# One decoder layer: the first two token groups projected without the row factor of RMSNorm, the factor multiplied in behind the projection

## The chip, the core and the metric

The kernel runs on one core of a Trainium2 chip. The metric is the device time of one execution in microseconds. The kernel before took 1266.46 us (median of three runs, 1264.92 to 1267.42). The core has five engines with one instruction queue each: TensorE (PE in the profile; PEld is its loading of weights), VectorE (DVE), ScalarE (ACT), GpSimd (POOL) and SyncE (SP), which issues most DMAs. TensorE writes to PSUM, in banks of 128 partitions by 512 words; the other engines copy results from there to SBUF.

## The reference, cut to what matters

```python
def rmsnorm(x, g):
    return x * rsqrt(mean(x * x, axis=-1) + EPS) * g

h = concatenate([meta, x])                      # 16 + 1024 tokens of 1024
a = rmsnorm(h, ln_mix_pre)
proj = a @ w_in                                 # 1024 x 3584
dq, dk, dv, hq, hf, hi, hg = split(proj)        # 7 kinds of 512 columns, 4 heads of 128 each
y_diff = diff_attention(dq, dk, dv, ...)        # relative-position bias, two softmaxes per head
y_hgrn = hgrn2(hq, hf, hi, hg, ...)             # gated linear recurrence, 4 heads
h = h + rmsnorm(concatenate([y_diff, y_hgrn]) @ w_out, ln_mix_post)
h = h + rmsnorm(conv_ffn(rmsnorm(h, ln_ffn_pre)), ln_ffn_post)
return h[16:]
```

All of it is f32. The factor `rsqrt(mean(x*x) + EPS)` is one number per token, the gain `g` one per column of x. Since the factor belongs to a token, `(x * g) @ w` may be multiplied by it afterwards; the gain may not.

## The kernel before, in words

**Precision.** Every f32 factor of a projection is split into a high part in the faster fp32r form and a low part, the rest. A projection is the sum of three products over eight slices k of 128 input columns: high weight by high x (`wh`, `ahi`), low weight by high x (`wl`, `ahi`), high weight by low x (`wh`, `alo`).

**Tokens.** The 1040 tokens (block 0 is the 16 meta rows, blocks 1 to 8 are 128 rows of x) form three groups: blocks 0 to 2 (272 tokens), 3 to 5 and 6 to 8 (384 each). Projections produce columns-by-tokens tiles: `pi_dq` is the PSUM accumulator of kind dq, one per group.

**The normed input.** x comes in twice. Its rows come as `x` (512 KB a block) and only serve to find the factors: the square and its sum per row (ScalarE with an accumulator, or DVE), then the reciprocal root on ScalarE. A transposed copy comes as `xr` (columns on the partitions), which is what TensorE needs. Since the factor there runs along the free dimension, it is spread over all partitions by TensorE: a diagonal matrix `dg` of the factors is multiplied with a matrix of ones into the PSUM tile `prs`. Then DVE forms `xr * gcol * prs` for each slice (`x_norm`, `gcol` is the gain), ScalarE casts it to `ahi`, and DVE or POOL subtracts to get `alo`. `ahi` and `alo` stay in SBUF for all 28 projection tiles.

**The start.** The loads are issued in a written order on SyncE's queue: blocks 1, 0, 2 of x, the first weight pieces (a kind has two of 256 KB; `wr` raw, cast into `wh` and `wl`) and group 0's transposed x, then blocks 3 to 5, the table for the position bias, group 1's transposed x, and later group 2's. Until the first data are there TensorE runs 26 and then 4 filler products of `ones`. Group 0's three kinds dq, dk, dv of head 0 come first, then group 1's, then group 2's. All instructions of this part keep the order in which they are written (the state "ordered"), on every engine. What a finished accumulator still needs is its evacuation, `out()`: for dq, ScalarE and DVE split it into the high and low parts of two half-heads (`q`); for dk the same into `k` and `kl`; for dv ScalarE copies it to `vt`, which TensorE later transposes into `avn` (`pn_va`, called by `flush()`). The position bias takes one product per head into PSUM (`pb`), a copy and a few steps on DVE.

**PSUM.** The start has eight banks: three tagged "ip" for the accumulators of groups 0 and 2, five tagged "m" for group 1's accumulators, `prs`, `pb`, `pn_va` and the fillers.

**The heads.** After the first three kinds the head stage begins with the projection `pi_hf` (it ends at about 470 us). It goes through four pairs of one attention head and one HGRN head; the projections of the next kind run between the steps of the current heads. Their evacuations go through the same functions: seven kinds in three groups per pair. Here DVE's, ScalarE's and POOL's order is set by a scheduler, TensorE's by the program.

**The rest.** From about 470 us on, the output projection, the convolutional feed-forward part and their norms run as before; the change does not touch them.

Of the kernel before, what the change touches and what calls it, by code (L numbers as in the profile page):

```python
# [36 lines left out]
WARM = 26  # L37
# [55 lines left out]
def layer_kernel(ctx: ExitStack, tc: tile.TileContext, x, meta, xt, relative, lbl, gpre, gpost, win,  # L93
# [23 lines left out]
    deep = {"ip": 3, "m": 5}  # L117
# [113 lines left out]
    at_p_cm, ap_ = pool("attn", 1, "right")  # L231
    z_cm, zp = pool("pre", 2, "right")
# [52 lines left out]
    def x_stats(g, on_vector=()):  # L285
        blks = range(*GROUPS[g])
        ss = zp.tile([P, 3], F32, tag="ss", name=f"ss{g}", bufs=3)
        if g == 0:
            V.memset(ss, 1.0)
        for c, i in sorted(enumerate(blks), key=lambda b: b[1] == 0):  # L290
            r = rows(i)
            if i in on_vector:
                V.tensor_tensor(x_rows[i][:r], x_rows[i][:r], x_rows[i][:r], op=ALU.mult)
                V.reduce_sum(ss[:r, c:c + 1], x_rows[i][:r], axis=AX.X)
            else:
                A.activation(x_rows[i][:r], x_rows[i][:r], AF.Square, accum_out=ss[:r, c:c + 1])
        rstd_of(ss, ss, D)
        res = {}
        for c, i in enumerate(blks):
            r = rows(i)  # L300
            res[i] = zp.tile([P, P], F32, tag="dg", name=f"dg{i}", bufs=3)
            if i in (1, 2, 3, 6):
                A.mul(res[i], ident, ss[:, c:c + 1])
            else:
                V.tensor_scalar(res[i][:r, :r], ident[:r, :r], ss[:r, c:c + 1], None, ALU.mult)
        return res

    def x_spread(g, stats):
        pt = ps_m(f"prs{g}")
        o = 0  # L310
        for i in range(*GROUPS[g]):
            r = rows(i)
            T.matmul(pt[:, o:o + r], ones[:r], stats[i][:r, :r], start=True, stop=True)
# [54 lines left out]
    def bias_table(h, tbb, oh):  # L368
        pt = ps_m(f"pb{h}")
        T.matmul(pt[:, :384], tbb[:, h], oh, start=True, stop=True)  # L370
        rb = zp.tile([P, 512], F32, tag=f"wv{h % 2}", name=f"rb{h}", bufs=1)[:, :384] if h > 1 else zp.tile([P, 384], F32, tag="rb", name=f"rb{h}", bufs=2)
# [34 lines left out]
    def hgrn_in(h):  # L406
# [15 lines left out]
        def ev_q(g, b0, b1, t0, t1, pt):  # L422
            A.mul(t["q"][:, t0:t1], pt, 128 ** -0.5)

        def ev_i(g, b0, b1, t0, t1, pt):
            ht = hp.tile([P, 384], F32, tag="ht", name=f"ht{h}_{g}", bufs=3)
            A.copy(ht[:, : t1 - t0], pt)
            late.append((t["vn"], ht, b0, b1, f"vh{h}_{g}"))

        def ev_g(g, b0, b1, t0, t1, pt):  # L430
            if g == 0:
                t["gate"] = hp.tile([P, L], F32, tag="gate", name=f"gate{h}")
            s = hp.tile([P, 384], F32, tag="sg", name=f"sg{h}_{g}")[:, : t1 - t0]
            sigmoid(s, s, pt)
            V.tensor_tensor(t["gate"][:, t0:t1], pt, s, op=ALU.mult)
# [196 lines left out]
    def attn_in(h):  # L632
# [8 lines left out]
        def ev_q(g, b0, b1, t0, t1, pt):  # L641
            for m in range(2):
# [4 lines left out]
        def ev_k(g, b0, b1, t0, t1, pt):  # L647
            for m in range(2):
# [158 lines left out]
    third = [ap_.tile([P, 4, 512], F32R, tag="pb", name=f"w3{c}", bufs=2) for c in range(2)]  # L807
# [17 lines left out]
    for i in (1, 0, 2):  # L825
        load_x(i)
    open_xt(1)
    load_raw(0, 0)
    load_xt(0, 0, 4)
    SY.dma_start(gcol, gpre)  # L830
# [4 lines left out]
    for i in (3, 4, 5):  # L835
        load_x(i)
    bias = spare[:64, 2 * D:2 * D + 388]
    SY.dma_start(bias, relative)
    for c in range(2):
        load_xt(1, 4 * c, 4 * c + 4)  # L840
    for c in range(2):
        for j in range(3):
            if j < 2:
                parts[j][c] = tuple(wp.tile([P, 512], F32R, tag=t, name=f"{t}_{tiles[j][1]}_{c}", bufs=4) for t in ("wh", "wl"))
            else:
                parts[j][c] = third[c][:, 0], third[c][:, 1]
# [35 lines left out]
    stats = x_stats(0, (0,))  # L882
    spread = {0: x_spread(0, stats)}
    keep_busy(warm, 4)
    w_hi(0, 0, G)
    w_lo(0, 0, G)
    w_hi(1, 0, G)
    w_lo(1, 0, G)
    for k in range(KD):
        x_norm(0, k, spread[0])  # L890
# [19 lines left out]
    for k in range(4):  # L910
        dq.mm(k, 0, ahi)
        dq.mm(k, 1, ahi)
        dk.mm(k, 0, ahi)
    for kd in (dq, dk):
        kd.part(1, 0, ahi)
    dk.part(0, 1, ahi)

    def low_parts(*ks):
        for k in ks:
            for kd in (dq, dk):  # L920
                kd.mm(k, 0, alo)

    for kd in (dq, dk):
        kd.part(1, 1, ahi)
    for half in range(2):
        dv.part(half, 0, ahi)
    low_parts(0, 1, 2, 3)
# [863 lines left out]
```

## Time and profile before

| | before |
|---|---|
| median of three runs | 1266.46 us (1264.92 to 1267.42) |
| the profiled execution | 1267.22 us |
| its span, first to last instruction | 1265.4 us |
| TensorE busy in the span | 1249.3 us (99%) |
| DVE, ScalarE, POOL busy | 911.9, 684.0, 512.9 us |
| mean granted TensorE clock | 0.998 |
| first product of a projection | at 11.69 us |
| head stage's first product (`pi_hf`) | at 51.08 us |

The span is what the profile sees; the execution's own time is 1.8 us longer. Times in the trace count from the span's start. In rows of an engine's order of time the columns are the start, the length, the engine, the line, the operation with its output and inputs by the program's names, the count of like instructions in a row, and in brackets how long the engine had waited ahead of it and for what. Line L60 is the helper through which every DVE, ScalarE and POOL operation passes, so those are told apart by their names; L863 is the product of a first-kind projection (`Kinds.mm`), L313 the spread product, L370 the bias product, L383 and L385 the transposes of dv, L250 to L254 the projections of the head stage.

### The profile page before, as it was taken

Reading aid. Unit: us, or ns where it says so; the run is one execution under the profiler, and the core shown is the slowest. Engines: PE = TensorE matmul, PEld = TensorE weight load, DVE = VectorE, ACT = ScalarE, POOL = GpSimd, SP = SyncE. Lnnn points to the kernel's source line nnn. Section 1 sums busy time; section 2 is a strip of 40 time slices with the busy share of each in tenths; the row PEclk is TensorE's granted clock in tenths of the full one; section 3 lists DMA queues with packets and bytes.
Section 4 is the critical chain, followed back from the end, with each engine's and each line's share of the span. In section 5 each row is a group of like instructions: output and inputs, shape, how many; then the busy total and the mean of one; then the engine's idle time right before and its main releaser. Section 6 shows DMA issues by size and latency. Waiting matters only on the chain.

```text
span 1265.4 us, 26124 instructions
## 1 busy us (share of the span) xinstructions
PE 1249.3 (99%) x10168; PEld 1169.8 (92%) x10168; DVE 911.9 (72%) x1505; ACT 684.0 (54%) x1632; POOL 512.9 (41%) x396
## 2 busy tenths in 40 slices
PE   9999999999999999999999999999999999999997
PEld 8999999999999998778999999999999998878886
DVE  6764646565655573557899888888898887797586
ACT  7765466547644764356764544445435454564554
POOL 5442323333313311353067676676776731020111
PEclk9999999999999999999999999999999999999999
DMA  8554564464634533787322221222222247955363
GB/s 323 171 105 100 97 140 84 98 125 116 117 100 68 126 88 123 235 276 262 114 68 71 89 93 59 101 76 76 94 76 83 76 130 269 354 171 166 92 217 125
DMA packets 117599, 169.30 MB, mean 134 GB/s; under 512 B 10258, under 2 KB 55122, under 8 KB 117476
## 3 DMA queue, kind: packets, MB, share of 16 engines
q1 hardware_dynamic: 94244, 156.10, 37.5%
q0 software_dynamic: 23232, 11.54, 7.7%
q8 instruction: 80, 1.31, 0.4%
q14 instruction: 43, 0.35, 0.1%
HBM read 138.50 MB, written 52.17 MB: 151 GB/s over the span
## 4 chain that ended last, share of the span: by engine, by line
PE 45%; DVE 5%; ACT 2%; issue 2%; POOL 1%; DMA 1%; SPq 0%; DVEq 0%; POOLq 0%; ACTq 0%
PE pd L1616 5%; PE pd L1617 5%; PE pd L1615 5%; PE pb L1438 4%; PE pb L1439 4%; PE pb L1440 4%; PE pa L1439 3%; PE pc L1440 3%; PE pa L1438 3%; PE pc L1439 3%; PE pc L1438 3%; PE pa L1440 3%; DVE t L60 1%; DVE xh L60 1%; DVE c L60 1%
## 5 line engine op out<-in xcount | busy, mean ns | idle before, releaser
L1438 PE MATMUL pb<-t,uh 128*128 128x258 f32 (+1 forms) x504 | 140.3, 278 | 0.9 <-DVE uu L60 0.9
L1439 PE MATMUL pb<-t,uh 128*128 128x258 f32 (+1 forms) x504 | 140.4, 279 | 0.4 <-DVE t L60 0.4
L1440 PE MATMUL pb<-t,ul 128*128 128x258 f32 (+1 forms) x504 | 139.9, 278 | 0.0
L1616 PE MATMUL pd<-wl,gh 128*128 128x512 f32 (+1 forms) x312 | 121.0, 388 | 1.7 <-DVE wl L60 1.7
L1615 PE MATMUL pd<-wh,gh 128*128 128x512 f32 (+1 forms) x312 | 120.7, 387 | 0.5 <-DVE x L60 0.5
L1617 PE MATMUL pd<-wh,gl 128*128 128x512 f32 (+1 forms) x312 | 120.7, 387 | 0.0
L60 ACT ACTIVATE c<-c 128x512 f32<-128x512 f32 x44 | 27.9, 634 | 150.5 <-DVE c L60 150.5
L60 DVE SCALAR_TENSOR_TENSOR c<-uu,cwt,c 128x512 f32<-128x512 f32 x88 | 105.6, 1200 | 0.0
L60 DVE SCALAR_TENSOR_TENSOR c<-ug,cwt,c 128x512 f32<-128x512 f32 x88 | 102.2, 1163 | 0.0
L1438 PEld LDWEIGHTS pb<-t,uh 128*128 128x128 f32 x504 | 94.7, 188 | 1.2 <-DVE uu L60 1.1
L60 POOL TENSOR_TENSOR ws<-ra,ra 128x512 f32<-128x512 f32 x42 | 70.7, 1682 | 61.9 <-DMA ra<-in_wup_dram 41.1
L1439 PEld LDWEIGHTS pb<-t,uh 128*128 128x128 f32 x504 | 94.8, 188 | 0.6 <-DVE t L60 0.6
L1440 PEld LDWEIGHTS pb<-t,ul 128*128 128x128 f32 x504 | 94.8, 188 | 0.0
L1439 PE MATMUL pa<-t,uh 128*128 128x258 f32 (+1 forms) x336 | 93.9, 279 | 0.0
L1438 PE MATMUL pa<-t,uh 128*128 128x258 f32 (+1 forms) x336 | 93.6, 278 | 0.0
L1440 PE MATMUL pa<-t,ul 128*128 128x258 f32 (+1 forms) x336 | 93.4, 278 | 0.0
L1438 PE MATMUL pc<-t,uh 128*128 128x256 f32 x336 | 92.8, 276 | 0.0
L1440 PE MATMUL pc<-t,ul 128*128 128x256 f32 x336 | 92.8, 276 | 0.0
L1439 PE MATMUL pc<-t,uh 128*128 128x256 f32 x336 | 92.8, 276 | 0.0
L60 POOL TENSOR_TENSOR ul<-ws,uh 128x512 fp32r<-128x512 f32 x42 | 68.7, 1637 | 58.8 <-PE pa L1440 43.7
L60 POOL TENSOR_TENSOR c<-c,c 128x512 f32<-128x512 f32 x44 | 66.5, 1511 | 50.2 <-ACT c L60 45.2
L60 DVE TENSOR_TENSOR ul<-ra,uh 128x512 fp32r<-128x512 f32 x43 | 41.5, 966 | 46.6 <-POOL ul L60 46.6
(386 smaller groups left out, 4178.5 us busy)
## 6 DMA issues: line engine op xcount, KB each, us to landing
ra<-in_wup_dram SPq DMA_DIRECT2D x88, 256.0 KB, 2.6
mp<-msc SPq DMA_DIRECT2D x23, 512.0 KB, 5.5
tsc<-in_wdown_dram SPq DMA_DIRECT2D x44, 256.0 KB, 4.9
gsc<-c SPq DMA_DIRECT2D x44, 256.0 KB, 2.2
wi<-tsc SPq DMA_DIRECT2D x44, 256.0 KB, 2.9
gi<-gsc SPq DMA_DIRECT2D x33, 256.0 KB, 4.8
wi<-in_wdown_dram SPq DMA_DIRECT2D x33, 256.0 KB, 5.2
tsc<-in_wdown_dram POOLq DMA_DIRECT2D x22, 256.0 KB, 6.7
```

The costliest lines, as they stand in the source:

```text
L60: ins = call(*args, **kw)
L1438: T.matmul(pt, hi[:, s], th[:, k], start=(first and k == 0), stop=False, skip_group_check=True)
L1439: T.matmul(pt, hi[:, s], tl[:, k], start=False, stop=False, skip_group_check=True)
L1440: T.matmul(pt, lo[:, s], th[:, k], start=False, stop=(k == 3), skip_group_check=True)
L1615: T.matmul(py, gh[:, s], wh, start=(k == 0 and pr not in (3, 7)), stop=False, skip_group_check=True)
L1616: T.matmul(py, gh[:, s], wl, start=False, stop=False, skip_group_check=True)
L1617: T.matmul(py, gl[:, s], wh, start=False, stop=(k == NH - 1), skip_group_check=True)
```

## The change

**Groups 0 and 1 are projected unnormed.** Their transposed x is multiplied by the gain alone (`x_gain`, DVE), cast and split, and projected. The factors are found meanwhile, spread over `prs` as before, and copied to a new SBUF tile `rt`. The multiplication comes at evacuation: `scaled` replaces a ScalarE copy (or copy with a constant) by a DVE product with `rt`; `scale`, for dq and dk, multiplies the accumulator in PSUM in place on DVE, ahead of the unchanged evacuation; the HGRN kinds hf and hg first write the product to SBUF. Because `ahi` and `alo` serve all projections, this holds for every one of the 28 tiles in groups 0 and 1. Group 2 is normed beforehand as it was.

**The loads.** The gain, half of group 0's transposed x and the first weight pieces come first; the rows of blocks 1, 2, 0 after the weights and half of group 1's transposed x; then its other half, the bias table, blocks 6 to 8 and group 2's transposed x, and blocks 3 to 5 last.

**Order and banks.** 15 fillers stand ahead of the first product in place of 26 and 4. Factors are found for group 0, then 2, then 1. "m" has two banks instead of five; a new tag "first" holds group 1's three accumulators. Group 1 is evacuated after group 2's high products.

The names are those of the tiles with a running number; a row can stand for several like instructions (x4). First, TensorE where group 1 of dq ends. Before:

```order
L313 MATMUL prs_459<-dg_441,ones 128x128
L313 MATMUL prs_459<-dg_443,ones 128x128
L313 MATMUL prs_459<-dg_445,ones 128x128
L863 MATMUL pi_dq_1_371<-alo,wh_dq_0_156 128x384 x4
L863 MATMUL pi_dq_1_371<-alo,wh_dq_1_160 128x384 x4
L383 MATMUL pn_va_0_495<-ident,vt_0_457 128x128
```

and now:

```order
L394 MATMUL pb_424<-oh,tbb 128x384
L893 MATMUL pi_dq_1_345<-alo,wh_dq_0_156 128x384 x4
L893 MATMUL pi_dq_1_345<-alo,wh_dq_1_160 128x384 x4
L334 MATMUL prs_441<-dg_398,ones 128x128
L334 MATMUL prs_441<-dg_400,ones 128x128
L334 MATMUL prs_441<-dg_402,ones 128x128
```

The spread product of group 2 (`prs_459`, now `prs_441`) moved behind the eight low products of dq; the bias product of head 0 (`pb_424`) stands directly ahead of them.

Second, DVE on the way to those diagonals `dg`. Before:

```order
L60 TENSOR_SCALAR dg_443<-ident,ss_435 128x128
L60 TENSOR_SCALAR dg_445<-ident,ss_435 128x128
L60 SCALAR_TENSOR_TENSOR q_0_118<-pi_dq_0_268,q_0_118 64x272
L60 SCALAR_TENSOR_TENSOR q_0_119<-pi_dq_0_268,q_0_119 64x272
L60 TENSOR_TENSOR kl_112<-pi_dk_0_269,k_0_120 64x272
L60 TENSOR_TENSOR kl_113<-pi_dk_0_269,k_0_121 64x272
```

and now (`ss` holds the factors, `rt` their spread copy in SBUF, `tbb` the bias table):

```order
L61 TENSOR_REDUCE ss_336<-x_130 128x1
L61 CAST tbb<-bias 64x512
L61 TENSOR_TENSOR tbb<-bias,tbb 32x512
L61 COPY rt<-prs_378 128x272
L61 TENSOR_TENSOR pi_dq_0_180<-pi_dq_0_180,rt 128x272
L61 SCALAR_TENSOR_TENSOR q_0_119<-pi_dq_0_180,q_0_119 64x272
L61 SCALAR_TENSOR_TENSOR q_0_120<-pi_dq_0_180,q_0_120 64x272
L61 TENSOR_TENSOR pi_dk_0_181<-pi_dk_0_181,rt 128x272
L61 TENSOR_TENSOR kl_113<-pi_dk_0_181,k_0_121 64x272
L61 TENSOR_TENSOR kl_114<-pi_dk_0_181,k_0_122 64x272
L61 TENSOR_SCALAR dg_400<-ident,ss_336 128x128
L61 TENSOR_SCALAR dg_402<-ident,ss_336 128x128
```

The two diagonals stood ahead of group 0's evacuation and stand behind it, and the evacuation has a copy and two multiplications more.

Third, TensorE at the end of group 2's high products, now, with the semaphores that each waits for in brackets:

```order
L334 MATMUL prs_554<-dg_532,ones 128x128 [waits DVE_49,PE_49,Activation_49]
L893 MATMUL pi_dq_2_491<-alo,wh_dq_1_160 128x384 [waits Pool_49] x4
L893 MATMUL pi_dk_2_492<-alo,wh_dk_1_162 128x384 x4
L394 MATMUL pb_593<-oh,tbb 128x384 [waits PE_49]
L394 MATMUL pb_599<-oh,tbb 128x384 [waits DVE_49]
L394 MATMUL pb_606<-oh,tbb 128x384 [waits DVE_49]
L409 MATMUL pn_va_1_613<-ident,vt_1_571 128x128 [waits DVE_49]
L893 MATMUL pi_dv_2_493<-alo,w_126 128x384 x4
```

The bias products of heads 1 to 3 (`pb`) moved from behind group 2's high products of dq and dk to behind their low ones, and group 1's spread product `prs_554` is new in this place; dv's low products follow the transposes `pn_va_1`.

The diff, cut to what these steps use:

```diff
-WARM = 26
+WARM = 15
+LATE = 2
...
-    deep = {"ip": 3, "m": 5}
+    deep = {"ip": 3, "m": 2}
...
+    def ps_first(name):
+        return pp.tile([P, 512], F32, tag="first", name=name, bufs=3)
...
+    rt = ap_.tile([P, 6 * P], F32, tag="rt", name="rt")
...
+    def scaled(g, t0, t1, dst, pt, by=None):
+        if g >= LATE:
+            A.copy(dst, pt) if by is None else A.mul(dst, pt, by)
+        elif by is None:
+            V.tensor_tensor(dst, pt, rt[:, t0:t1], op=ALU.mult)
+        else:
+            V.scalar_tensor_tensor(dst, pt, by, rt[:, t0:t1], ALU.mult, ALU.mult)
+
+    def scale(g, t0, t1, pt):
+        if g < LATE:
+            V.tensor_tensor(pt, pt, rt[:, t0:t1], op=ALU.mult)
...
+    def x_gain(g, k):
+        return V.tensor_scalar(xr[g][:, k], xr[g][:, k], gcol[:, k:k + 1], None, ALU.mult)
...
         def ev_q(g, b0, b1, t0, t1, pt):
+            scale(g, t0, t1, pt)
             for m in range(2):
                 A.mul(qs[m][own[m], t0:t1], pt[own[m]], 0.125)
...
-            A.copy(vt[:, : t1 - t0], pt)
+            scaled(g, t0, t1, vt[:, : t1 - t0], pt)
...
+    for k in near:
+        x_gain(0, k)
+        x_hi(0, k)
+    for j in range(2):
+        w_hi(j, 0, G)
+        w_lo(j, 0, V)
...
+    for k in near:
+        x_gain(1, k)
+        x_hi(1, k)
+        x_lo(1, k, G)
+    x_square(1)
+    x_square(2)
+    x_square(0, V)
...
+    x_diag(0, (1, 2))
+    x_square(6, V)
+    tbb = bias_casts(bias)
+    x_square(7)
+    tbb = tbb, one_hot(bias)
+    second = [Kinds(j, 1, ps_first) for j in range(3)]
     for k in range(KD):
         for kd in second:
             kd.mm(k, 0, ahi)
             kd.mm(k, 1, ahi)
+        if k == 4:
+            spread = x_spread(0)
+            V.tensor_copy(rt[:, slice(*span(0))], spread)
+            dq.out()
+            dk.out()
+            x_square(8)
+            x_diag(2, (6,))
+            dv.out()
+    bias_table(0, *tbb)
...
+    each(range(KD), second[0], a=alo)
+    spread = x_spread(2)
     for k in range(KD):
+        last_norm = x_norm(2, k, spread)
         last_hi = x_hi(2, k)
         x_lo(2, k, G)
...
+    for i in (3, 4, 5):
+        x_square(i)
+    x_diag(1, (3,))
+    each(range(KD), dv)
+    each(range(KD), dv, w=1)
+    spread = x_spread(1)
+    V.tensor_copy(rt[:, slice(*span(1))], spread)
+    for kd in second:
+        kd.out()
+    for kd in third:
+        each(range(KD), kd, a=alo)
+        if kd is dk:
+            for h in range(1, HEADS):
+                bias_table(h, *tbb)
             flush()
+        kd.out()
```

More of the change, by code (lines that the diff above doesn't have):

```diff
@@ L417, in ev_f @@
             fs = t["f"][:, t0:t1]
+            if g < LATE:
+                scaled(g, t0, t1, t["kr"][:, t0:t1], pt)
+                pt = t["kr"][:, t0:t1]
             sigmoid(fs, t["kr"][:, t0:t1], pt)
@@ L806, in layer_kernel @@
     t_a, tiles = attn_in(0)
-    third = [ap_.tile([P, 4, 512], F32R, tag="pb", name=f"w3{c}", bufs=2) for c in range(2)]
+    wv3 = [ap_.tile([P, 4, 512], F32R, tag="pb", name=f"w3{c}", bufs=2) for c in range(2)]
     far = [mix_tile("X0", F32, "x0")]
@@ L823, in load_raw @@
         SY.dma_start(raws[j, c], win[tiles[j][0]][:, 512 * c: 512 * (c + 1)])
-    for i in (1, 0, 2):
-        load_x(i)
     open_xt(1)
+    open_xt(2)
+    SY.dma_start(gcol, gpre)
+    load_xt(0, 0, 4)
     load_raw(0, 0)
-    load_xt(0, 0, 4)
-    SY.dma_start(gcol, gpre)
     load_raw(1, 0)
@@ L834, in layer_kernel @@
         load_raw(j, c)
-    for i in (3, 4, 5):
+    load_xt(1, 0, 4)
+    for i in (1, 2, 0):
         load_x(i)
-    bias = spare[:64, 2 * D:2 * D + 388]
+    load_xt(1, 4, 8)
     SY.dma_start(bias, relative)
-    for c in range(2):
-        load_xt(1, 4 * c, 4 * c + 4)
     for c in range(2):
@@ L845, in layer_kernel @@
             else:
-                parts[j][c] = third[c][:, 0], third[c][:, 1]
+                parts[j][c] = wv3[c][:, 0], wv3[c][:, 1]
     def w_hi(j, c, eng):
@@ L881, in layer_kernel, with each @@
     keep_busy(warm, WARM)
[L882 to L890, printed above, removed]
+    dq, dk, dv = first = [Kinds(j, 0, ps_in) for j in range(3)]
+    def each(ks, *kds, w=0, a=ahi):
+        for k in ks:
+            for kd in kds:
+                kd.mm(k, w, a)
+    near, far_ = range(4), range(4, KD)
+    for k in near:
+        x_gain(0, k)
@@ L891, in layer_kernel @@
         x_hi(0, k)
     for j in range(2):
-        w_hi(j, 1, G)
+        w_hi(j, 0, G)
+        w_lo(j, 0, V)
+    for k in near:
+        x_lo(0, k, G)
+    each(near, dq)
+    each(near, dk)
+    each(near, dq, w=1)
+    each(near, dk, w=1)
+    each(near, dq, dk, a=alo)
+    for k in far_:
+        x_gain(0, k)
+        x_hi(0, k)
+    for j in range(2):
+        w_hi(j, 1, V)
+        w_lo(j, 1, V)
     for c in range(2):
         w_hi(2, c, A)
-    for j in range(2):
-        w_lo(j, 1, V)
@@ L898, in layer_kernel @@
-    for k in range(4):
+        w_lo(2, c, G)
+    for k in far_:
         x_lo(0, k, V)
-    for c in range(2):
-        w_lo(2, c, V)
-    for k in range(4, KD):
-        x_lo(0, k, V)
+    each(far_, dq)
+    each(far_, dq, w=1)
+    each(far_, dk)
+    each(near, dv)
+    each(far_, dk, w=1)
+    each(far_, dv)
+    each(near, dv, w=1)
+    each(near, dv, a=alo)
+    each(far_, dq, dk, a=alo)
+    each(far_, dv, w=1)
+    each(far_, dv, a=alo)
+    for k in near:
+        x_gain(1, k)
+        x_hi(1, k)
+        x_lo(1, k, G)
@@ L904, in layer_kernel @@
+    x_square(1)
+    x_square(2)
+    x_square(0, V)
+    for i in (6, 7, 8):
+        load_x(i)
+    for c in range(2):
+        load_xt(2, 4 * c, 4 * c + 4)
+    for k in far_:
+        x_gain(1, k)
+        x_hi(1, k)
+        x_lo(1, k, G)
     for m in range(2):
         G.memset(az[m], 0.0)
+    x_diag(0, (1, 2))
+    x_square(6, V)
     tbb = bias_casts(bias)
-    stats = x_stats(1)
+    x_square(7)
     tbb = tbb, one_hot(bias)
-    dq, dk, dv = first = [Kinds(j, 0, ps_in) for j in range(3)]
@@ L910, in layer_kernel @@
[L910 to L927, printed above, removed]
-    for half in range(2):
-        dv.part(half, 1, ahi)
-    low_parts(4, 5, 6, 7)
@@ L931, in layer_kernel @@
-    spread[1] = x_spread(1, stats)
-    for half in range(2):
-        dv.part(half, 0, alo)
-    x_norm(1, 0, spread[1])
-    x_hi(1, 0)
-    for k in range(1, KD):
-        x_norm(1, k, spread[1])
-        x_hi(1, k)
-    for k in range(KD):
-        x_lo(1, k, G)
-    second = [Kinds(j, 1, ps_m) for j in range(3)]
+    second = [Kinds(j, 1, ps_first) for j in range(3)]
     for k in range(KD):
```

105 lines of the change are left out of this document (45 added, 60 removed).

## The prediction

> **What bounds the kernel now.** I read the page first, then TensorE's order of time over the first 75 us, then the waits of the other engines there.
>
> ```profile
> span 1265.4 us, 26124 instructions
> PE 1249.3 (99%) x10168; PEld 1169.8 (92%) x10168; DVE 911.9 (72%) x1505; ACT 684.0 (54%) x1632; POOL 512.9 (41%) x396
> ```
>
> TensorE has work in 1249.3 of 1265.4 us, so whatever delays it anywhere is paid in full, and only its start and its few waits can be won. The change touches the first 51 us, and the evacuation of every projection after that. In TensorE's order of time (start, length, what it writes, count, and in brackets the wait ahead):
>
> ```profile
> 11.69 0.36 PE L863 MATMUL pi_dq<-ahi,wh_dq 128*128 128x272 f32 x1 [0.24 <-ACT ahi L60]
> 20.92 0.94 PE L313 MATMUL prs<-dg,ones 128*128 128x128 f32 x6
> 34.21 0.27 PE L383 MATMUL pn_va<-ident,vt 128*128 128x128 f32 x1
> 37.33 0.34 PE L863 MATMUL pi_dq<-ahi,wh_dq 128*128 128x384 f32 x1
> 42.97 0.79 PE L370 MATMUL pb<-oh,tbb 64*128 64x384 f32 x3
> 43.99 1.63 PE L863 MATMUL pi_dq<-alo,wh_dq 128*128 128x384 f32 x8
> 46.85 2.98 PE L863 MATMUL pi_dv<-ahi,w 128*128 128x384 f32 x16
> 51.08 0.29 PE L250 MATMUL pi_hf<-ahi,wh_hf 128*128 128x272 f32 x1
> ```
>
> The first useful product starts at 11.69. By 34.21 groups 0 and 1 are through but for the low parts of dk and dv; at 37.33 group 2 begins, and at 51.08 the head stage. Of those 39.4 us almost none is waiting.
>
> **The start.** The row factors no longer stand ahead of the first product. It needs gcol, half of group 0's transposed x (128 rows of 1088 words, 544 KB) and one weight piece: 4 + 544 + 256 = 804 KB.
>
> ```profile
> x<-in_x_dram SPq DMA_DIRECT2D x7, 512.0 KB, 6.5
> xr<-in_xt_dram SPq DMA_DIRECT2D x2, 768.0 KB, 10.3
> 4.81 1.06 ACT L60 ACTIVATE x<-x 128x1024 f32<-128x1024 f32 x1 [2.80 <-DMA x<-in_x_dram]
> 7.48 0.61 POOL L60 CAST wh_dq<-wr_dq 128x512 fp32r<-128x512 f32 x1 [3.77 <-DMA wr_dq<-in_win_dram]
> 18.71 1.06 ACT L60 ACTIVATE xm<-xm 128x1024 f32<-128x1024 f32 x1 [1.02 <-DMA xm<-in_x_dram]
> ```
>
> Before, the first 512 KB were there at 4.81 and the first 1344 KB (two blocks, meta, one weight piece) at 7.48; 804 KB lie at 5.75 between them. POOL's cast adds 0.61, and the four high parts about as much beside it: first product at about 6.7, a **gain of 5.0 us**. Fewer fillers (15) cost nothing if they end before that.
>
> **The first pause.** The gain lasts only as long as nothing later waits. Group 1's second half of x is the 14th load; ahead of it and with it stand the same bytes as up to block 5 before (two pieces of 768 KB for three blocks of 512 KB), and block 5 was there at 18.71. So it lands at 18.7 whatever TensorE does. After it, DVE and ScalarE work in a written order, with these lengths:
>
> ```profile
> 5.05 1.22 DVE L60 TENSOR_TENSOR xm<-xm 16x1024 f32<-16x1024 f32 x1 [4.18 <-DMA xm<-in_meta_dram]
> 6.30 1.21 DVE L60 TENSOR_REDUCE ss<-xm 16x1 f32<-16x1024 f32 x1
> 19.09 0.42 DVE L60 CAST tbb<-xm 64x512 fp32r<-64x512 f32 x1
> 19.55 0.68 DVE L60 TENSOR_TENSOR tbb<-xm,tbb 32x512 fp32r<-32x512 f32 x1
> 30.06 0.56 DVE L60 COPY rb<-pb 128x384 f32<-128x384 f32 x1 [3.88 <-PE pb L370]
> 31.58 0.89 DVE L60 SCALAR_TENSOR_TENSOR q<-pi_dq,q 64x272 fp32r<-64x272 f32 x2
> 33.41 4.29 DVE L60 SCALAR_TENSOR_TENSOR xr<-xr,gcol,prs 128x384 f32<-128x384 f32 x8
> 40.98 1.12 DVE L60 SCALAR_TENSOR_TENSOR q<-pi_dq,q 64x384 fp32r<-64x384 f32 x2
> 68.53 0.43 DVE L60 TENSOR_TENSOR S<-S,rr 128x256 f32<-128x256 f32 x1
> 28.73 1.05 ACT L60 ACTIVATE x<-x 128x1024 f32<-128x1024 f32 x1
> 29.89 0.30 ACT L60 ACTIVATE ss<-ss,eps 128x3 f32<-128x3 f32 x1
> 30.46 0.40 ACT L60 ACTIVATE dg<-ident,ss 128x128 f32<-128x128 f32 x1
> 30.77 0.78 ACT L60 ACTIVATE q<-pi_dq 64x272 fp32r<-64x272 f32 x2
> 32.26 0.86 ACT L60 CAST k<-k 64x272 fp32r<-64x272 f32 x2
> 34.06 4.19 ACT L60 CAST ahi<-xr 128x384 fp32r<-128x384 f32 x8 [0.53 <-DVE xr L60]
> 38.57 0.98 ACT L60 ACTIVATE q<-pi_dq 64x384 fp32r<-64x384 f32 x2
> 40.45 1.05 ACT L60 CAST k<-k 64x384 fp32r<-64x384 f32 x2
> 46.67 0.62 ACT L60 CAST wh_hf<-wr_hf 128x512 fp32r<-128x512 f32 x1
> ```
>
> The new multiplication in PSUM has its nearest row at 68.53 (0.43 for 256 columns in place): I take 0.45 for 272 columns and 0.56 for 384, the copy's own price at 30.06; 0.43 and, as two half-width passes would be, 1.12 (40.98) are its ends.
>
> ScalarE casts four high parts (4.19/8 each) until 21.1, has group 0's factors at 21.7 (29.89 to 30.46 is 0.57), and the spread product prs0 starts near 22.4. DVE, in order: square of block 6 from 21.7 (1.25 + 1.21) to 24.2; the two tbb steps to 25.3; copy of the factors and dq's multiplication to 26.3; ScalarE's q half to 26.7; two q steps to 27.6; dk's multiplication to 28.05; ScalarE's four k casts (0.78 + 0.86) to 29.7. Only then stands block 8's square in ScalarE's queue (28.73 to 29.89: 1.16), to 30.9, then 0.57 and 0.40: **group 2's diagonals at 31.9**. TensorE reaches the product prs2 much sooner: 22.4, 0.6 for prs0, three columns of group 1 (18 products at (51.08 - 46.85)/24 = 0.176, so 3.2), 0.3 for pb, 1.4 for eight low products: 27.9. It stands for 4.0 us. I count some ten handovers in this chain at nothing; at 0.1 each the pause is 5. With 4.6, TensorE passes its point of 34.21 at about 33.2: of the 5.0 us 1.0 is left.
>
> **The second pause.** From 33.2, 3.1 us (34.21 to 37.33) lead to group 2 at 36.3, dq and dk take 5.64 (37.33 to 42.97) and dv's high and low weights 2.8: 44.7. The factors of group 1 need blocks 3 to 5, squared by ScalarE after group 2's casts: eight norms from 34.9 (4.29) and the last cast to 39.8, transposes' copies 0.5, three squares 3.3, then 0.3, 0.57, 0.40: 44.8, so prs1 is hardly late and ends at 45.4. Now the evacuation of group 1 starts, where before it was done by 43. DVE: copy 0.56 and multiplication 0.56 to 46.5; ScalarE first casts wh_hf into the buffer that dq's low products free at 46.8, to 47.4, then q to 47.9; DVE's q steps 1.12 to 49.0, dk's multiplication to 49.6; ScalarE casts three weight pieces (0.52 each, 46.67 on) and k by 50.5; kl 1.12 and vt 0.56 to 52.2; ScalarE's k copies and q of group 2 to 52.6; DVE's q steps to 53.7; only then the copy of pb1, to 54.3. With two banks left under "m" (five before), pb3 needs that bank: TensorE, there at 45.4 + 2.86 (43.99 to 46.85) + 0.4 = 48.7, **stands 5.6 us**, and pn_va_1 another 1.0 for pb2's copy. Behind them stand dv's last eight products (1.4): the head stage opens at 57.1, with handovers at 0.1 at 57.6. **Sum of the front: +6.5 us** (51.08 to 57.6); ends +2 (each queue 2 us quicker) and +10 (a multiplication at 1.12, handovers of 0.2).
>
> **The heads.** Seven kinds times two groups of multiplications per pair of heads put about 1.0 us per kind on DVE, 25 us in all over 420, and take some copies from ScalarE.
>
> ```profile
> 51.00:140.00 89.00, 88.90 (x854) 86.37 (x853) 52.29 (x120) 50.74 (x148) 26.00 (x26) 1.00 0.44 104
> 186.84 0.28 DVE L60 COPY at<-pt 128x128 f32<-128x128 f32 x1
> 187.04 0.48 DVE L60 SCALAR_TENSOR_TENSOR pb<-pb,ast 128x272 f32<-128x272 f32 x1
> 188.91 0.97 DVE L60 TENSOR_REDUCE ast<-S 128x2 f32<-128x800 f32 x1
> 188.40 0.39 PE L760 MATMUL pa<-avn,at 128*128 128x128 f32 x2
> ```
>
> DVE is busy 59% here (52.29 of 89) and TensorE waits 0.1 us, so most of the 25 us hides. The tight place is the copy "at" of token block 1: done at 187.12, used at 188.40, 1.28 us of room. In the changed order of heads 1 to 3 it stands behind the three steps that follow it now (187.04 to 188.91, 1.87 us) and one multiplication more (0.56): late by 0.6 to 1.1 each, 2.6 in all, and 0.7 for the first head: **+3.3**, ends 0 and +9 (2 us a head and the first).
>
> **Sum.** -5.0 at the start; +4.6, +5.6 and +1.0 of pauses, smaller terms inside the front's +6.5; +3.3 in the heads: +9.8. The profiled span 1265.4 becomes 1275.2, its execution 1267.22 becomes 1277.0, and the median of the runs, 0.8 below that execution, 1266.46 + 9.8 = **1276.3 us**.
>
> **Rivals.** *The clock falls in the pauses.* The first fillers ran at half pace:
>
> ```profile
> 2.00:4.00 2.00, 2.00 (x12) 2.00 (x11) 0.00 (x0) 0.01 (x1) 1.66 (x3) 1.00 0.85 317
> 6.00:7.00 1.00, 1.00 (x12) 1.00 (x11) 0.97 (x2) 0.69 (x1) 0.00 (x0) 1.00 1.03 344
> ```
>
> Twelve records in two microseconds, later twelve in one, so for some 3.5 us after 1.27. If each pause brings that back, each costs half of 3.5: +3.5, **1279.8**. For it: no wait on TensorE before is near 4 us, so nothing shows the clock surviving one. Against: the pauses may be shorter than what it takes. [...]
>
> *The heads swallow their multiplications:* only the front counts, 1266.46 + 6.5 = **1273.0**. DVE's 41% of free time speaks for it, the moved copy against.
>
> *Faster.* The mechanism is the handing round between DVE and ScalarE before prs2 and pb3: if ScalarE and DVE really overlap there, so that the pauses come to less than about 5 us together in place of 11.2, the start's 5 us survive. At 2 us in all the front gains 3 and the heads give nothing back: **1263.5**. Against it: both queues are served in order and the rows' lengths fill them.
>
> *No effect:* pauses of about 5 us eat just the start's gain, 1266.5. That the first product does not start earlier at all belongs to the forecast's upper end, since group 1's load binds anyway.
>
> **How the numbers follow.** Forecast 0.48, clock 0.22, heads swallowed 0.14: slower 0.84. Faster 0.10. Within 0.2% (2.5 us, what this measurement can tell from nothing) 0.06. The range 1268 to 1286 leaves out the faster and most unchanged cases and about 0.05 above, for clock and heads at their ends together.
>
> **What would show it.** Right: the first pi_dq near 6.7; TensorE waiting 4 to 5 us at prs of group 2, 5 to 6 us at the third pb; pi_hf first at 57 to 58; 0.5 to 1.5 us at pa once per head. Wrong: pi_hf before 51, or waits under 3 us at both places; records of half pace behind the pauses would make the clock rival right.

## The result, and the profile after

The changed kernel takes 1286.06 us (median of four runs, 1285.9 to 1286.68), the kernel before, beside it, 1266.94: a ratio of 1.0152, 95% interval 1.0134 to 1.0170, or 19.1 us (17.0 to 21.5). The direction was forecast, the size not: 9.8 were forecast, and 1286.06 lies just past the range's upper end, 1286.0.

The profiled span grew by 18.5 us, from 1265.4 to 1283.9. TensorE's busy time grew by 2.0 of them, from 1249.3 to 1251.3; the other 16.5 it stood still. From the page of the changed kernel:

```profile
span 1283.9 us, 26097 instructions
PE 1251.3 (97%) x10138; PEld 1170.3 (91%) x10138; DVE 945.7 (74%) x1563; ACT 670.7 (52%) x1606; POOL 519.6 (40%) x398
```

TensorE's order of time over the front, with the landmarks that the prediction used:

```profile
7.04 0.75 PE L893 MATMUL pi_dq<-ahi,wh_dq 128*128 128x272 f32 x4
...
19.19 0.34 PE L893 MATMUL pi_dq<-ahi,wh_dq 128*128 128x384 f32 x1
...
25.27 1.03 PE L334 MATMUL prs<-dg,ones 16*128 16x16 f32 x6 [0.68 <-DVE dg L61]
...
30.39 1.66 PE L893 MATMUL pi_dq<-alo,wh_dq 128*128 128x384 f32 x8
36.87 1.51 PE L334 MATMUL prs<-dg,ones 128*128 128x128 f32 x6 [4.83 <-ACT dg L61]
...
42.27 0.42 PE L893 MATMUL pi_dq<-ahi,wh_dq 128*128 128x384 f32 x1
...
60.27 0.69 PE L394 MATMUL pb<-oh,tbb 64*128 64x384 f32 x1 [5.38 <-DVE rbs L61]
...
61.76 2.83 PE L893 MATMUL pi_dv<-alo,w 128*128 128x384 f32 x8
64.42 0.29 PE L255 MATMUL pi_hf<-ahi,wh_hf 128*128 128x272 f32 x1
```

Both pauses stand where they were forecast, 4.83 and 5.38 us long. But eight low products of dv that took 1.56 us before take 2.83 behind the second. The trace records each change of the granted clock: here at 37.05, 40.46, 57.53 and 64.36. The stretches below are 3.4 us long, as long as the first stay at half clock (37.05 to 40.46), and laid along these changes, to within 0.1 us (columns: stretch, its length, busy us and count of PE, PEld, DVE, ACT, POOL, then granted clock, DMA share, GB/s):

```profile
30.25:33.66 3.41, 1.79 (x9) 1.34 (x8) 1.90 (x5) 1.31 (x4) 0.80 (x3) 1.00 1.00 403
33.66:37.06 3.40, 0.19 (x1) 0.19 (x2) 1.49 (x5) 3.01 (x8) 0.00 (x0) 1.00 0.11 32
37.06:40.46 3.40, 3.40 (x14) 3.40 (x14) 3.31 (x8) 1.37 (x3) 0.80 (x1) 0.50 0.19 59
40.46:43.87 3.41, 3.41 (x22) 3.38 (x21) 3.16 (x7) 3.33 (x9) 3.41 (x5) 1.00 0.50 94
54.08:57.48 3.40, 0.81 (x4) 0.29 (x2) 2.32 (x5) 3.27 (x7) 3.17 (x4) 1.00 0.45 117
57.48:60.88 3.40, 0.61 (x1) 0.28 (x1) 3.07 (x8) 0.97 (x2) 1.89 (x3) 0.51 0.66 221
60.88:64.28 3.40, 3.15 (x12) 3.08 (x12) 2.41 (x8) 2.06 (x5) 0.00 (x0) 0.50 0.90 229
```

The clock is 0.50 behind the first pause for one such stretch, 3.41 us; at the second it falls within the pause and stays at 0.50 for two, 57.53 to 64.36. TensorE's waits over the whole changed kernel (total us, times, longest):

```profile
PE pb L394 <- DVE rbs L61: 5.4, 1, 5.4
PE prs L334 <- ACT dg L61: 4.8, 1, 4.8
PE pl L521 <- DVE hq L61: 3.1, 2, 1.5
PE pl L521 <- issue: 2.2, 2, 1.2
...
PE pa L793 <- DVE at L61: 0.5, 3, 0.2
```

"issue" marks a wait for nothing that the profile shows. In the heads TensorE waits at `pl`, the level products of the HGRN head (line 521), in each of heads 1 to 3 once (1.53, 1.17 and 1.54 us), and hardly at `pa` behind the copy "at". DVE's order of time at the first such place, after:

```profile
146.57 0.63 DVE L61 TENSOR_TENSOR pi_dq<-pi_dq,rt 128x384 f32<-128x384 f32 x1
148.24 1.12 DVE L61 SCALAR_TENSOR_TENSOR q<-pi_dq,q 64x384 fp32r<-64x384 f32 x2 [1.05 <-ACT q L61]
149.40 0.70 DVE L61 TENSOR_TENSOR kr<-kr,tt 128x520 f32<-128x520 f32 x1
150.01 1.77 DVE L61 TENSOR_TENSOR hq<-hq,tt 128x520 f32<-128x520 f32 x1
```

and before, 13.4 us earlier as the whole stage is:

```profile
133.93 1.12 DVE L60 SCALAR_TENSOR_TENSOR q<-pi_dq,q 64x384 fp32r<-64x384 f32 x2 [1.23 <-ACT q L60]
135.08 0.70 DVE L60 TENSOR_TENSOR kr<-kr,tt 128x520 f32<-128x520 f32 x1
135.70 0.69 DVE L60 TENSOR_TENSOR hq<-hq,tt 128x520 f32<-128x520 f32 x1
```

The multiplication of `pi_dq` ends at 147.2; only then can ScalarE take its half of q, DVE stands 1.05 us for it, and the level's own step `hq` lies behind all that in DVE's queue. It is done at 151.78 instead of 136.39 + 13.4 = 149.8, 0.9 of it by queue and 1.1 by its own longer run. TensorE waits 1.53 us for it at 151.93. Beside the longer run stands POOL's subtraction for the next weights, begun 0.21 us earlier:

```profile
149.80 1.43 POOL L61 TENSOR_TENSOR wl_dv<-wr_dv,wh_dv 128x512 fp32r<-128x512 f32 x1 [10.28 <-ACT wh_dv L61]
```

It ended at 151.23, and `hq` 0.55 us behind it. Before, this subtraction began at 136.91, when `hq` was done. So the later place in the queue cost twice: 0.9 us by itself, and 1.1 in the longer run beside POOL. The third of the three heads repeats it (`hq` 1.77 us long at 398.20, POOL's subtraction 1.44 from 397.97); in the second `hq` took 0.70.

Up to the head stage 13.3 us are lost (51.08 to 64.42), up to the output projection's first product 19.3 (489.89 to 509.2), so 6.0 in the heads. The 0.8 us that the span gains back behind it are less than executions of one kernel differ. (The head stage lasts until that product; the 470 us told above for its end is too early.)

### The profile page after: what moved, and what is told of

It reads as the page before. It is cut to its first block, busy times and chain, and to the rows that moved or that the text cites. A ratio compares the mean times of both kernels' runs of the same rounds, so it can differ in the third digit from the quotient of the medians.

```text
span 1283.9 us, 26097 instructions
## 1 busy us (share of the span) xinstructions
PE 1251.3 (97%) x10138; PEld 1170.3 (91%) x10138; DVE 945.7 (74%) x1563; ACT 670.7 (52%) x1606; POOL 519.6 (40%) x398
## 4 chain that ended last, share of the span: by engine, by line
PE 42%; DVE 5%; DMA 3%; ACT 2%; issue 1%; POOL 1%; SPq 1%; DVEq 0%; ACTq 0%; POOLq 0%
PE pb L1478 4%; PE pb L1479 4%; PE pb L1480 4%; PE pd L1656 4%; PE pd L1657 4%; PE pd L1655 4%; PE pa L1479 3%; PE pc L1478 3%; PE pa L1478 3%; PE pc L1480 3%; PE pc L1479 3%; PE pa L1480 3%; DMA gi<-gsc 1%; DVE t L61 1%; DVE xh L61 1%
## 5 line engine op out<-in xcount | busy, mean ns | idle before, releaser
L61 ACT ACTIVATE c<-c 128x512 f32<-128x512 f32 x44 | 27.9, 634 | 151.8 <-DVE c L61 151.8
L61 POOL TENSOR_TENSOR c<-c,c 128x512 f32<-128x512 f32 x44 | 65.4, 1485 | 52.4 <-ACT c L61 50.4
```

Of the source, the lines that this page charges most:

```text
L61: ins = call(*args, **kw)
```

## The experiments

Each run is compared with runs of the kernel before on the same chip; their medians lay between 1266.63 and 1267.30. The intervals of the ratios are some 4 us wide for most runs, as wide as some of the differences; where two variants are told apart by less, the landmarks of their profiles do it, and a profile is of one execution.

**Does the clock, or something else, slow the work behind the pauses?** Fillers in both pauses:

```diff
         pt = ps_m(f"prs{g}")
+        keep_busy(pt, 20 if g == 2 else 0)
...
             for h in range(1, HEADS):
+                if h == 3:
+                    keep_busy(second[0].pt, 20)
                 bias_table(h, *tbb)
```

> Both pauses of TensorE stay, but 20 filler products run at the start of each (20 products of two records each, at twelve records per us 3.3 us), so that TensorE stands still for only some 1.5 and 2 us. Theory A (after each pause the granted clock is 0.5 for some 3.5 us, and that costs 1.8 us behind the first and 1.6 us behind the second): the pauses end where they did, the work behind them runs at full pace, the head stage's first product comes at about 61.1 instead of 64.4, and the time falls by 3.3 us against the changed kernel, to about 1282.7. Theory B (the products behind the pauses are slow for another reason, such as operands that come late): the clock in the windows behind the pauses and the head stage's start stay as they are, time 1286.

Measured 1282.73 us, ratio 1.0121 (1.0106 to 1.0136). TensorE's order with the fillers (L909):

```profile
31.79 4.63 PE L909 MATMUL prs<-ones 128*128 128x128 f32 x40
36.79 0.94 PE L335 MATMUL prs<-dg,ones 128*128 128x128 f32 x6 [0.37 <-ACT dg L61]
...
53.37 4.73 PE L909 MATMUL pi_dq<-ones 128*128 128x128 f32 x40
58.65 0.43 PE L395 MATMUL pb<-oh,tbb 64*128 64x384 f32 x1 [0.55 <-DVE rbs L61]
```

The first pause ends where it did (36.79 against 36.87), so the fillers bought nothing there; but the granted clock stays at 1.00 through both pauses and behind them, and the head stage starts at 61.8. The clock was 2.6 us of the front by the profiles, 3.3 by the medians, as theory A has it. The 20 fillers took 4.63 and 4.73 us, not 3.3, so they filled nearly the whole of each pause.

**What holds the first pause?**

```diff
             spread = x_spread(0)
+            x_square(8)
+            x_diag(2, (6,))
             V.tensor_copy(rt[:, slice(*span(0))], spread)
             dq.out()
             dk.out()
-            x_square(8)
-            x_diag(2, (6,))
```

> Block 8's square and group 2's diagonals stand ahead of group 0's evacuation, on ScalarE in the 4 us in which it idles there (26.8 to 30.9). Theory A (the first pause is that evacuation's handing round between DVE and ScalarE, standing ahead of the diagonals in both queues): the wait at the spread product of group 2 goes from 4.8 to under 0.5 us, and the half clock behind it goes with it (1.8 us). But the norms and casts of group 2 are next in DVE's queue, behind group 0's evacuation that still is there; they give back about 3 us as waits of 1 to 1.6 us at the first products of group 2. Head stage at about 60.8, time about 1282.5. Rival (the whole pause is won, the norms are early enough): head stage at 57.9, time 1279.5. Rival (the pause is the landing of block 8): nothing moves, 1286.

Measured 1281.91 us, ratio 1.0120 (1.0102 to 1.0137). TensorE's order:

```profile
31.62 0.83 PE L334 MATMUL prs<-dg,ones 128*128 128x128 f32 x6
36.69 0.33 PE L407 MATMUL pn_va<-ident,vt 128*128 128x128 f32 x1 [1.43 <-DVE rbs L61]
...
38.18 0.69 PE L893 MATMUL pi_dq<-ahi,wh_dq 128*128 128x384 f32 x1 [0.94 <-ACT ahi L61]
```

The wait at the spread product is gone; block 8 had landed long before, for ScalarE squared it at 26.45 in this run. About half of it comes back as 1.43 and 0.94 us at what follows, for group 0's evacuation still stands ahead of the norms. Group 2 starts 4.1 us earlier (38.18 against 42.27), the head stage 2.6 (61.8). The granted clock fell again all the same, to 0.50 from 37.89 to 41.3, and the second pause stayed at 5.39 us.

**What holds the second pause?**

```diff
             kd.mm(k, 1, ahi)
+        if k in (2, 4, 6):
+            bias_table(k // 2, *tbb)
...
         if kd is dk:
-            for h in range(1, HEADS):
-                bias_table(h, *tbb)
             flush()
```

> The bias products of heads 1 to 3 stand between group 2's high products again, where DVE has time for their copies. Theory A (the second pause is the evacuation of group 1, which cannot start before its factors are there, and the third bias product only happens to stand behind it): the wait moves on to the transposes of dv of group 1, which need the last step of that evacuation, 4 to 5 us there; the half clock stays; head stage about 1.2 us earlier, time about 1284.8. Theory of the prediction taken at its word (the third product waits because only two banks are left under that tag): the 5.4 us and the 1.6 us of half clock behind them vanish, head stage at about 57.5, time about 1279.

Measured 1284.65 us, ratio 1.0139 (1.0122 to 1.0157). In TensorE's order of time the wait has moved on to the transposes:

```profile
60.77 0.55 PE L409 MATMUL pn_va<-ident,vt 128*128 128x128 f32 x3 [4.13 <-DVE vt L61]
```

So the two banks under "m" only decided which product stood there. The head stage starts at 63.07, 1.35 us earlier. Both moves together, with dv evacuated first (the products at k = 3, 5, 7 here):

```diff
-    for kd in second:
+    for kd in second[2:] + second[:2]:
         kd.out()
```

> Both moves together (block 8's square and the diagonals ahead of group 0's evacuation; the bias products of heads 1 to 3 between group 2's high products), and in the evacuation of group 1 dv first, so that the transposes of dv no longer wait for its end. Theory A (what TensorE waits for at the end of the front is the whole evacuation of groups 1 and 2, which starts only when group 1's factors are spread, near 51 us, and which DVE and ScalarE need some 10 us for): the 5.4 us go from the third bias product and from the transposes, but 4 us come back at the head stage's first products, which need PSUM banks that this evacuation frees; half clock follows there. Time about 1280.3, 1.6 below the run with the first move alone. Rival (the queue order was the whole cause, nothing is behind it): both pauses gone, head stage from about 54 at full clock, time about 1275.

Measured 1282.48 us, ratio 1.0115 (1.0095 to 1.0135): by the medians no better than the first move alone. In the list of TensorE's waits it reappears at the head stage's first product:

```profile
PE pi_hf L255 <- ACT avn L61: 3.6, 1, 3.6
```

The head stage starts at 58.07 there, 6.3 us earlier than in the changed kernel, but at a granted clock of 0.50 until 61.1. This profile is of the shortest of the four executions (1279.32); the others took 1281.89 to 1283.91, and what they did otherwise was not profiled. What the run shows is that TensorE waits for the evacuation of groups 1 and 2, wherever its next dependent product stands.

**The heads: order, load, or the copy "at"?** First, heads 1 to 3 without the query's multiplication:

```diff
         def ev_q(g, b0, b1, t0, t1, pt):
-            scale(g, t0, t1, pt)
+            if h == 0:
+                scale(g, t0, t1, pt)
```

> Leaves out the multiplication by the row factor for the query projections of heads 1 to 3 (six in-place products of DVE in all, 0.43 or 0.63 us each), so that those queries lack the factor of groups 0 and 1. All else stays. Theory A (in the heads TensorE loses 1.5 us three times at the HGRN head's level products, because DVE's product, ScalarE's half of the query and DVE's two steps on it stand in DVE's queue ahead of the level's own step): those waits fall under 0.3 us each and the time falls by 4 to 4.8 us to about 1281.7. Theory of the prediction (the loss is the copy of token block 1's attention weights, behind steps that follow it in DVE's order): the loss stays, time within 0.6 us of 1286. Rival (DVE's mean load from all multiplications): a quarter of the loss, 1.2 us, goes.

Measured 1281.33 us, ratio 1.0117 (1.0100 to 1.0134). From the list of TensorE's waits in the heads, where the long one at `pl` is gone and that for "at" is what it was:

```profile
PE pa L794 <- DVE at L61: 0.5, 3, 0.2
PE pl L521 <- issue: 0.2, 1, 0.2
```

The output projection's first product comes 4.5 us earlier (504.7 against 509.2). Of the 6.0 us of the heads, six of the fifty multiplications there (18 in attention heads 1 to 3, 32 in the HGRN heads) carry 4.5, and the wait at `pl` for `hq`, 3.1 us at two places in the changed kernel, is no longer in the list. The same six, by a tile of ones, added to the kernel before (with the bias rows of heads 0 and 1 in another buffer, to make room for the tile):

```diff
         def ev_q(g, b0, b1, t0, t1, pt):
+            if h and g < 2:
+                V.tensor_tensor(pt, pt, rt[:, t0:t1], op=ALU.mult)
```

> Made from the kernel before, whose front stays as it is: in heads 1 to 3 DVE multiplies the query projections of groups 0 and 1 in place by a tile of ones (six products of 0.43 or 0.63 us; the result is the same). Theory A (that product and the handing round behind it, ahead of the HGRN level's step in DVE's queue, are the loss of the heads): TensorE waits three times 1.2 to 1.5 us at the level products, time 1266.9 + 4.3 = about 1271.2. Rival (the loss comes from all seven kinds' multiplications together): under 1 us, 1267.5.

Measured 1271.72 us against 1266.63, ratio 1.0039 (1.0024 to 1.0054), with this row in the list of TensorE's waits:

```profile
PE pl L492 <- DVE hq L60: 4.6, 3, 1.5
```

So three waits for `hq` are 4.6 of the 5.1 us that this run takes longer.

And all multiplications kept, with only the order changed (the evacuation of the query's group 1 is issued behind the next HGRN level, and its two DVE steps after that level's `hq`):

```diff
+            with tc.issue_after(ends["v"].ins) if h and g == 1 else nullcontext():
                 for m in range(2):
                     V.scalar_tensor_tensor(qs[m][oth[m], t0:t1], pt[own[m]], 0.125, ...
...
             level(lev)
+            if held:
+                held.pop()()
```

> All multiplications stay; in heads 1 to 3 only the order of DVE changes: for the query projection of group 1, DVE's two steps on ScalarE's half stand behind the HGRN head's level step, where they stood ahead of it. Theory A (order, not load): the three waits of 1.2 to 1.5 us at the level products go, as with the multiplications left out, and the time falls by 4 to 4.5 us to about 1281.7. Rival (DVE simply has too much work there): the waits stay or move to the next level's products, time within 1 us of 1286.

Measured 1281.77 us, ratio 1.0107 (1.0088 to 1.0125); of the waits at `pl` in the heads 0.6 us is left, and none of it for `hq`. In the profiles the heads take 441.4 us (65.4 to 506.8), in the changed kernel 444.8 (64.42 to 509.2), before 438.8: 3.4 of the 6.0 are back, with every multiplication in place. So most of the loss is the order of DVE's queue, with what `hq` met there, and not DVE's load.

**Why was the front later than forecast even ahead of the first pause?** POOL without the eight subtractions of group 1:

```diff
         x_gain(1, k)
         x_hi(1, k)
-        x_lo(1, k, G)
+        G.memset(alo[:, k, cols(1)].bitcast(F32), 0.0)
```

> Leaves out the low parts of group 1's x (POOL sets them to zero, 0.1 to 0.3 us each, in place of eight subtractions that took 12.3 us from 18.5 to 30.7); TensorE's products all stay. Between 18.5 and 30 DVE's steps took longer than the same steps before: 2.03 against 1.22 us for the meta rows' square, 0.97 against 0.42 and 1.38 against 0.68 for the bias table. Theory A (DVE and POOL slow one another there): these go back to 1.2, 0.42 and 0.68, the diagonals of group 0 come 0.8 us and those of group 2 about 2 us earlier; the head stage starts about 2 us earlier, time about 1284, give or take 1.7 us for where the clock's changes fall. Rival (they are slow for another reason, a DMA or their data): the lengths stay, time 1286.

Measured 1284.76 us, ratio 1.0140 (1.0124 to 1.0156). DVE's order of time in the changed kernel:

```profile
18.76 2.03 DVE L61 TENSOR_TENSOR x<-x 16x1024 f32<-16x1024 f32 x1
...
24.62 0.60 DVE L61 TENSOR_SCALAR dg<-ident,ss 16x16 f32<-16x16 f32 x1 [1.27 <-ACT ss L61]
...
27.51 0.97 DVE L61 CAST tbb<-bias 64x512 fp32r<-64x512 f32 x1
28.52 1.38 DVE L61 TENSOR_TENSOR tbb<-bias,tbb 32x512 fp32r<-32x512 f32 x1
```

The same steps without POOL's subtractions:

```profile
20.11 1.21 DVE L61 TENSOR_TENSOR x<-x 16x1024 f32<-16x1024 f32 x1
...
25.19 0.22 DVE L61 TENSOR_SCALAR dg<-ident,ss 16x16 f32<-16x16 f32 x1 [1.32 <-ACT ss L61]
...
27.71 0.41 DVE L61 CAST tbb<-bias 64x512 fp32r<-64x512 f32 x1
28.16 0.68 DVE L61 TENSOR_TENSOR tbb<-bias,tbb 32x512 fp32r<-32x512 f32 x1
```

The lengths go back as theory A has it, 2.5 us in all. The place in time did not follow in full: DVE came to the meta rows' square later (20.11 against 18.76), group 0's diagonals came 0.6 us later, not 0.8 earlier, and group 2's product came 1.06 us earlier (35.81 against 36.87) instead of 2. Half of that expectation missed. The trace shows a likely reason: POOL's eight zeroing steps, 0.41 us each, started between 15.8 and 18.3, ahead of that place, and beside them DVE's four multiplications of group 1's first half by the gain took 3.09 us from 17.09 on, where they took 1.40 in the changed kernel. So both runs have steps of DVE that took longer beside POOL, and by my estimate 1.06 us understates what the subtractions cost in the changed kernel.

**Can the change be saved?** All repairs together, with fillers where TensorE still waits:

> Both moves of the front, dv first, the changed order in the heads, and 12 and 20 filler products at the two places of the front at which TensorE still waits, against the half clock. Theory A by its parts: 1280.3 of the front, less 4.4 in the heads, less 3 of clock: about 1273, still some 5 us slower than the kernel before, because the evacuation of group 1 is late and DVE and ScalarE have more to do in the front than before. Rival (nothing but order and clock was wrong with the change): the start's 4.65 us show up, time near 1263.

Measured 1275.18 us, ratio 1.0059 (1.0043 to 1.0075): 8.3 us above the kernel before. The last 20 fillers ran from 57.32 to 61.7, when the head stage's first product followed without a wait; in the run with both moves alone it had started at 58.07. The granted clock fell once more, to 0.50 from 48.6 to 52.0. Then the smaller step, made from the kernel before: only group 0 without its factor, group 1's rows loaded ahead of group 0's, the start as in the change.

> Made from the kernel before: only group 0 is projected without the row factor. Groups 1 and 2 are normed ahead as before; blocks 3 to 5 and group 1's transposed x are loaded ahead of blocks 1, 2 and 0; five banks under 'm' stay, 15 fillers, the start's order of the changed kernel. Theory A (TensorE's early start is worth only what DVE and ScalarE can follow, and they fill 20 to 44 us of the kernel before almost entirely): group 0 starts near 7, group 1 near 20.5, and by group 2 the lead is gone, since the added copy and three multiplications stand ahead of group 2's norms in DVE's queue; head stage at 53 to 55 instead of 51.1, heads about 1 us longer, time about 1271. Rival (group 1's late factor was what spoiled the change, and without it the start's gain stays): head stage at 48, time about 1264.

Measured 1270.93 us, ratio 1.0035 (1.0023 to 1.0048). Group 1 starts 2.4 us earlier than before (20.68 against 23.11), and then the lead is gone at group 0's factors, in TensorE's order of time:

```profile
20.68 0.45 PE L890 MATMUL pi_dq<-ahi,wh_dq 128*128 128x384 f32 x1 [0.75 <-ACT ahi L61]
...
28.69 1.72 PE L330 MATMUL prs<-dg,ones 16*128 16x16 f32 x6 [2.51 <-DVE dg L61]
```

Group 2 starts at 41.27 against 37.33, after a wait of 2.51 and 6.8 us at a granted clock of 0.50 behind it (28.4 to 35.2). The head stage starts at 55.1, 4.0 us later than before, and that is nearly all that this version loses. No version tried beats the kernel before.

## Why the prediction was wrong, point by point

*What bounds the kernel* held: TensorE's busy time moved by 2 us of 1250, and the time grew by what it stood still.

*The start* was right: 7.04 for a forecast of 6.7. But the prediction had no term for group 0's own time. Its 72 products took 12.15 us (7.04 to 19.19), where 72 x 0.125 would be 9.0 (the products start 0.12 to 0.13 us apart where none of them waits, as from 17.19 on); before, group 0 took 11.42 (11.69 to 23.11), with a spread product in it. Three waits of 0.3 to 0.6 us, for casts and subtractions of DVE and POOL, stand between the products. Of the lead of 4.65 us at the first product 3.92 were left where group 1 starts.

*The first pause* was right in place, in the chain behind it and in length (4.83 for 4.6), but both its ends came later. It ends when group 2's diagonals are there: at 36.82, not at 31.9. The step that failed is "ScalarE casts four high parts (4.19/8 each) until 21.1". The last of these casts ended at 24.1, 3.0 us late:

```profile
20.82 1.21 DVE L61 TENSOR_REDUCE ss<-x 16x1 f32<-16x1024 f32 x1
...
22.39 1.75 ACT L61 CAST ahi<-xr 128x384 fp32r<-128x384 f32 x4 [0.66 <-DVE xr L61]
```

The second half of group 1's x landed at 19.96, not at 18.7; that is 1.3 of the 3.0. The rest is DVE, which the sum took to be free. It had had no wait since 9.64 and came to those four slices only at 21.96, behind the meta rows' square and sum (18.76 to 22.03). The prediction took the lengths of the square and of the bias table's steps from rows of the kernel before (5.05, 19.09, 19.55) beside which POOL was idle. Now five steps of DVE between 9.64 and 20.79 took 4.0 us longer beside POOL than the same steps alone: two multiplications by the gain (0.94 and 0.86 for 0.35), a subtraction of weights (1.66 for 0.69), one of x (1.53 for 0.43) and the meta rows' square (2.03 for 1.21). By these rows I estimate that DVE alone would have been ready when the x landed; of the five, only the last was tried in a run.

Behind the casts, block 0's diagonal, which the sum left out and which took 0.60 beside POOL, added 0.4, the bias table's two steps 1.3, and the handing round took 6.9 us for 6.6. TensorE came to the pause at 32.0 (36.87 - 4.83) and not at 27.9, and here 2.2 of the 4.1 us are its own: it reached group 0's spread product at 24.6, where the prediction had it ready before 22.4. Then it stood 0.68 us for the diagonals and 0.61 for the bias table. That the length came out right, with both ends late and only in part for the same reason, is partly luck.

*The second pause* was right in length (5.38 for 5.6), and so was the chain added up for it: from the spread product's end to the third bias product 8.7 us for 8.9. But 'With two banks left under "m" (five before), pb3 needs that bank' gave only the place: with the product moved, the wait followed to the transposes and then to the head stage.

*The sum of the front* was +6.5 and came out at +13.3. The excess of 6.8 is 4.4 at the end of the first pause (36.87 for 27.9 + 4.6), and most of the rest is the clock, which had been set apart as a rival.

*The rival of the clock* was therefore right in what it said would happen (a granted clock of 0.50 at both pauses) and in price (3.5 forecast; 2.6 to 3.3 measured), and wrong in standing beside the forecast instead of in it; its time of 1279.8 missed for the same terms as the forecast's. The argument against it, that the pauses might be too short, no row of the kernel before could settle; pauses of 4.83 and 5.38 us proved long enough. In the changed kernel the clock changes at 37.05, 40.46, 57.53 and 64.36, so it stood at 0.50 for 3.41 us and for 6.83.

*The heads*, +3.3 at the copy "at", came out at +6.0, and the place was wrong: "at" cost 0.5, the HGRN level step 4.5; the last 1.0 stays open. The step that failed is 'The tight place is the copy "at" of token block 1', which looked only around the attention head's own chain. The handing round that the prediction priced in the front (DVE's product, ScalarE's half, DVE's two steps) stands in the heads as well, and what is queued behind it there had no term.

*Heads swallowed* and *faster* fell: both queues do hand round one after the other, and the waits stayed at 10.2 us in all.

## What to carry to other kernels

A lead of the bottleneck engine at the start is worth only what the engines behind it can follow; here DVE had no room in the front, without a wait from 9.64 to 23.35, and each of the three orders tried gave the lead back at another product. When a step is made longer on an engine that also serves another stream, look at what stands behind it in that engine's queue everywhere it occurs, not only in its own chain, and at what another engine does when the delayed step runs (`hq` took 1.77 us for 0.69 beside POOL's subtraction). And the two pauses of TensorE here, 4.83 and 5.38 us, had a second price in the granted clock of 0.50 behind them, 2.6 to 3.3 us for both: where a kernel's trace shows such a fall, add it to the sum.

## What the runs showed of the hardware

**The granted clock, and how long TensorE was busy before it changed.** In the run with block 8's square moved ahead no single wait near 38 us was longer than 1.43 us, and the clock fell at 37.89 (columns and stretches as above):

```profile
34.45:37.85 3.40, 1.36 (x8) 0.79 (x6) 2.96 (x8) 1.32 (x4) 0.00 (x0) 1.00 0.00 0
37.85:41.25 3.40, 3.07 (x10) 3.08 (x11) 3.40 (x9) 3.33 (x7) 3.05 (x4) 0.51 0.40 100
```

With the bias products moved, the same view:

```profile
55.11:58.51 3.40, 1.53 (x9) 1.21 (x7) 1.79 (x4) 3.21 (x7) 2.92 (x4) 1.00 0.25 78
58.51:61.91 3.40, 1.14 (x8) 1.15 (x9) 2.62 (x5) 2.93 (x7) 2.17 (x2) 1.00 0.54 167
61.91:65.32 3.41, 3.41 (x15) 3.41 (x14) 1.27 (x3) 2.26 (x5) 0.00 (x0) 0.50 0.83 252
```

Behind the stretch with 1.53 us busy the clock was 1.00, behind the one with 1.14 it was 0.50. Over all stretches laid out in this way, those at full clock with 0 to 1.36 us busy and one with 1.74 were followed by half clock, those with 1.53, 1.79 and more by full clock; 1.53 and 1.74 stand the wrong way round, and the busy times are modelled, so these runs show no exact line. Of the stretches at half clock, those with 0.61 to 3.08 us busy were followed by another at half clock, those with 3.07 to 3.41 by full clock. With both moves of the front, waits of the same 1.43 and 0.94 us at the same place fell into two stretches with 1.97 and 2.47 us busy, and the clock stayed at 1.00. The half clock at the first pause lasted 3.41 us in the changed kernel and 6.8 in the runs with the bias products moved, with DVE's order changed in the heads and without POOL's subtractions.

**DVE and POOL beside one another.** Four DVE steps took 4.98 us beside POOL's subtractions and 2.52 in the run without them. Instruction by instruction, the meta rows' square began at 18.76, while a subtraction of POOL ran until 19.71, and ended at 20.79, 1.08 us behind it; without the subtractions it took 1.21. Block 6's square began at 25.13, 0.01 us ahead of POOL's next subtraction: it took its 1.21 us in both runs, and the subtraction 2.08. So two squares that take 1.21 us each without the subtractions took 2.03 and 1.21 beside them. In these two pairs the step that began second was the long one; but at 21.96 DVE's multiplications by the gain took 0.40 each beside a subtraction begun at 21.63, and that one took 2.60. POOL's subtraction of 384 columns took 1.54 us on average in that stretch (12.29/8) and 0.98 in the kernel before, from 23.13 on (7.85/8). In the heads of the changed kernel the same shows twice: `hq` took 1.77 us in place of 0.69 and ended 0.55 and 0.56 us behind POOL's subtraction.
